# First projections of the two MLPs: feature tiles 8 to 31 by seven products of half-size matrices

## The chip, the cores and the metric

The kernel runs on one core of one Trainium2 chip. The metric is the device time of one execution in microseconds, the median of several executions. A profile is one execution with the hardware profiler on.

## What is computed

The program is a decoder trunk of two residual layers over 512 tokens with 1024 channels. Each layer has a token mixer (gated linear attention and block-sparse attention in the first layer, a short convolution and a pooling mixer in the second) and an MLP with 4096 hidden features. All data is float32. The change touches the MLPs alone:

```python
def rmsnorm(x, g):
    y = x * lax.rsqrt(jnp.mean(x * x, axis=-1, keepdims=True) + EPS)
    return y * g

def mlp(h, w1, w2):                       # w1: (1024, 4096), w2: (4096, 1024)
    a = jax.nn.relu(h @ w1)
    return (a * a) @ w2

for i in range(2):
    x = x + mix_i(rmsnorm(x, norm_mix[i]))
    x = x + mlp(rmsnorm(x, norm_mlp[i]), w1[i], w2[i])
```

## The kernel before

Activations lie transposed: channels on the 128 partitions, the 512 tokens along the free axis, so x is eight tiles of 128x512. The norm's gain is applied before the projection and its scale per token (rs) after it, since the scale is the same for all channels of a token.

**Three matmuls for one product.** Every float32 operand is kept as two float32r parts, hi (a rounded copy) and lo (the rest). `mm3` (L129 to L132) issues three matmuls for one product of tiles: hi times hi (L130), hi times lo (L131), lo times hi (L132). Each has a 128x128 stationary operand (the weights, loaded by a weight load of its own) and 512 moving columns.

**Weight blocks.** The weights come from HBM as blocks of 128x1024 float32 (512 KB) in exactly the order in which PE uses them. `block_parts` (L101) makes one block: SP issues the load into a `raw` buffer (L113), ScalarE casts it to `whi` (L114), VectorE subtracts that from `raw` into `wlo` (L115). There are four buffers each of raw, whi and wlo. `wblock` (L122) gives PE the next block and has two more emitted ahead of it. So ScalarE and VectorE make a block while PE works on earlier ones, and each queue works strictly in its own order.

**The MLP** (`mlp`, from L306). Hidden features are 32 tiles of 128. A unit of the first projection (`t_unit`) makes two feature tiles over eight channel tiles: 2 x 8 x 3 = 48 matmuls of 512 columns from two weight blocks, into one of two PSUM tiles `mm` (two banks each). Its evacuation is four instructions: `r` = max(o, 0) x rs on VectorE (L331), the square on ScalarE (L332), the cast to hi on ScalarE (L334), the subtraction to lo on VectorE (L335). The parts go to slots in A or in E. Four units are a group of eight tiles (`m1(g)`), and a down projection `m2(g)` takes the eight tiles of group g into x: four units of 48 matmuls, each followed by one addition to x (`x_add`, L292). The order is m1(0), m1(1), m2(0), m1(2), m2(1), m1(3), m2(2), m2(3). The last unit of the last MLP is cut into three pieces, the last two of 256 columns, and each piece is added to x (L347) and stored (L348).

**The norm ahead of an MLP.** `Norm.step` splits x times gain into A for each channel tile (hi on ScalarE, lo on VectorE, L259 and L260) and sums squares on POOL (L273). `norm_rs` splits that sum (L278, L279) and has PE add it over the partitions (L280, L281); PE's queue holds these two matmuls behind the MLP's first unit.

Within an MLP POOL has nothing to do before the change.

Of the kernel before, what the change touches and what calls it, by code (L numbers as in the profile page):

```python
# [40 lines left out]
C_N = 128  # L41


@with_exitstack
def kernel(
# [57 lines left out]

    def block_parts(n):
        i = wcount[0]
# [12 lines left out]
    def emit_block():  # L118
        for _ in block_parts(1):
            pass  # L120

    def wblock():  # L122
        while len(ready) < AHEAD + 1 and wcount[0] < w.shape[0]:
            emit_block()
        return ready.pop(0)
# [180 lines left out]
    def mlp(l, nrm, nxt):  # L306
        with ExitStack() as c2:
            mp = c2.enter_context(tc.tile_pool(name=f"mp{l}", bufs=2, reuse_waits="tile"))
            E = mp.tile([P, 16, S], F32R, tag="E", name=f"E{l}", bufs=1)
            st = {}  # L310

            def aslot(f):
                i = f % 8
                if (f // 8) % 2 == 0:
                    return A[:, 16 + i, :], A[:, 24 + i, :]
                return E[:, i, :], E[:, 8 + i, :]

            def apair(f):
                i = f % 8
                if (f // 8) % 2 == 0:  # L320
                    return A[:, 16 + i : 18 + i, :], A[:, 24 + i : 26 + i, :]
                return E[:, i : i + 2, :], E[:, 8 + i : 10 + i, :]

            def m1(g):
                for q in range(4):
                    f = 8 * g + 2 * q
                    o = t_unit(f"m1_{l}_{f}", H)
                    if "rs" not in st:
                        st["rs"] = nrm.rs()
                    r = mp.tile([P, 2, S], F32, tag="r", name=f"r_{l}_{f}")  # L330
                    dve.scalar_tensor_tensor(r, o, 0.0, bc2(st["rs"]), op0=ALU.max, op1=ALU.mult)  # L331
                    act.activation(r, r, AF.Square)  # L332
                    hi, lo = apair(f)
                    act.copy(hi, r)  # L334
                    dve.tensor_sub(lo, r, hi.bitcast(F32))  # L335

            def last_unit(g, n):
                ws = [[t.rearrange("p (k n) -> p k n", k=4) for t in wblock()] for _ in range(2)]
                for j, c0, c1 in ((0, 0, S), (1, 0, S // 2), (1, S // 2, S)):
# [7 lines left out]
                    dve.tensor_add(x[:, row, c0:c1], x[:, row, c0:c1], o[:, c0:c1])  # L347
                    nc.sync.dma_start(out[row * P : (row + 1) * P, c0:c1], x[:, row, c0:c1])  # L348

            def m2(g):  # L350
                for n in range(4):
# [3 lines left out]
                    o = mm_tile(f"m2_{l}_{g}_{n}")  # L355
                    for b in range(2):
# [16 lines left out]

            m1(0)
            m1(1)
            m2(0)
            m1(2)
            m2(1)
            m1(3)
# [724 lines left out]
```

## Time and profile before

| | us |
|---|---|
| median of 3 runs | 1081.18 (1079.22 to 1081.26) |
| profiled execution, its own time | 1080.98 |
| its span, first to last instruction | 1079.2 |
| PE busy in it (matmuls) | 1072.1 |
| PEld busy (weight loads, beside matmuls) | 885.7 |
| DVE busy (VectorE) | 546.0 |
| ACT busy (ScalarE) | 411.7 |
| POOL busy (GpSimd) | 102.4 |

The rows of matmuls are pipelined: one reads 0.39 us long while the next starts 0.23 us after it. What a matmul costs is therefore read from start to start. The same holds in a smaller measure for ScalarE and VectorE, whose rows overlap by about a tenth of a microsecond when they follow each other without a wait. "Landing" of a transfer is the time from the start of its issue to its completion.

### The profile page before, as it was taken

What the parts mean: (1) busy time and instruction counts of PE and PEld (TensorE: products, weight loads), DVE (VectorE), ACT (ScalarE), POOL (GpSimd) and SP (SyncE); (2) the same over time, 40 slices, a digit from 0 to 9 for tenths busy, and PEclk for the clock granted to TensorE, in tenths of its full rate; (3) what the DMA queues carried; (4) which work ended last, traced back from release to release, by engine and by line L of the source; (5) the groups of instructions that cost most, each with busy time, mean ns of one, the idle gap of its engine ahead of it and who ended that gap; (6) DMA issues with size and microseconds to landing.
All of it is one profiled execution on the core that took longest, in us unless ns stands there. A gap on an engine that the chain in (4) does not pass through costs nothing.

```text
span 1079.2 us, 12499 instructions
## 1 busy us (share of the span) xinstructions
PE 1072.1 (99%) x4970; PEld 885.7 (82%) x4970; DVE 546.0 (51%) x767; ACT 411.7 (38%) x597; POOL 102.4 (9%) x113
## 2 busy tenths in 40 slices
PE   9999999999999999999999999999999999999998
PEld 7778888788888888888888888888888888888887
DVE  7788885676444344334334864555443344344331
ACT  6565575755342133124123333334342133133110
POOL 0244432012000000000002100121000000000000
PEclk9999999999999999999999999999999999999999
DMA  8123123123322323333233232332333322322221
GB/s 305 43 78 103 54 90 126 60 78 98 98 98 98 98 98 98 97 98 98 98 98 98 89 97 98 98 98 98 98 98 98 97 98 97 96 96 94 94 72 59
DMA packets 31179, 104.77 MB, mean 97 GB/s; under 512 B 3633, under 2 KB 4498, under 8 KB 31122
## 3 DMA queue, kind: packets, MB, share of 16 engines
q1 hardware_dynamic: 30050, 101.46, 28.8%
q0 software_dynamic: 640, 2.10, 0.6%
q8 instruction: 39, 0.64, 0.3%
q10 hardware_dynamic: 432, 0.42, 0.1%
q14 instruction: 18, 0.15, 0.0%
HBM read 101.87 MB, written 2.10 MB: 96 GB/s over the span
## 4 chain that ended last, share of the span: by engine, by line
PE 95%; DVE 2%; ACT 1%; DMA 0%; issue 0%; DVEq 0%; ACTq 0%
PE m L130 22%; PE m L132 22%; PE m L131 21%; PE wo L130 1%; PE wo L132 1%; PE wo L131 1%; PE av L726 1%; PE ptp L707 1%; PE kb L130 1%; PE kb L132 1%; PE kb L131 1%; PE va L130 1%; PE va L132 1%; PE xc L130 1%; PE va L131 1%; PE xc L132 1%
## 5 line engine op out<-in xcount | busy, mean ns | idle before, releaser
L114 ACT CAST whi<-raw 128x1024 fp32r<-128x1024 f32 (+1 forms) x188 | 194.1, 1034 | 528.0 <-PE m L131 432.0
L115 DVE TENSOR_TENSOR wlo<-raw,whi 128x1024 fp32r<-128x1024 f32 (+1 forms) x188 | 227.2, 1209 | 191.6 <-ACT whi L114 191.5
L132 PE MATMUL m<-A,wlo 128*128 128x512 f32 x768 | 298.8, 389 | 0.0
L131 PE MATMUL m<-A,whi 128*128 128x512 f32 x768 | 298.8, 389 | 0.0
L130 PE MATMUL m<-A,whi 128*128 128x512 f32 x768 | 298.8, 389 | 0.0
L132 PEld LDWEIGHTS m<-A,wlo 128*128 128x128 f32 x768 | 144.2, 188 | 30.1
L130 PEld LDWEIGHTS m<-A,whi 128*128 128x128 f32 x768 | 144.2, 188 | 29.8
L131 PEld LDWEIGHTS m<-A,whi 128*128 128x128 f32 x768 | 144.2, 188 | 29.7
L131 PE MATMUL m<-E,whi 128*128 128x512 f32 (+1 forms) x264 | 101.0, 383 | 0.0
L132 PE MATMUL m<-E,wlo 128*128 128x512 f32 (+1 forms) x264 | 101.0, 383 | 0.0
L130 PE MATMUL m<-E,whi 128*128 128x512 f32 (+1 forms) x264 | 101.0, 383 | 0.0
L292 DVE TENSOR_TENSOR x<-x,m 128x1024 f32<-128x1024 f32 x31 | 37.8, 1221 | 109.1 <-PE m L132 109.1
L331 DVE SCALAR_TENSOR_TENSOR r<-m,rs_n 128x1024 f32<-128x1024 f32 x32 | 39.2, 1224 | 96.8 <-PE m L132 96.8
L273 POOL TENSOR_TENSOR ss_n<-ss_n,sq_n 128x512 f32<-128x512 f32 x21 | 32.8, 1561 | 418.5 <-ACT sq_n L271 417.8
L131 PEld LDWEIGHTS m<-E,whi 128*128 128x128 f32 x264 | 49.6, 188 | 9.8
L132 PEld LDWEIGHTS m<-E,wlo 128*128 128x128 f32 x264 | 49.6, 188 | 9.7
L130 PEld LDWEIGHTS m<-E,whi 128*128 128x128 f32 x264 | 49.6, 188 | 9.5
L332 ACT ACTIVATE r<-r 128x1024 f32<-128x1024 f32 x32 | 34.0, 1062 | 19.9 <-DVE r L331 19.9
L335 DVE TENSOR_TENSOR E<-r,E 128x1024 fp32r<-128x1024 f32 x16 | 19.6, 1226 | 17.2 <-ACT E L334 17.2
L260 DVE SCALAR_TENSOR_TENSOR A<-x,vc,A 128x512 fp32r<-128x512 f32 x24 | 27.3, 1140 | 1.3
L335 DVE TENSOR_TENSOR A<-r,A 128x1024 fp32r<-128x1024 f32 x16 | 19.6, 1225 | 15.1 <-ACT A L334 15.1
L131 PE MATMUL wo<-A,whi 128*128 128x512 f32 x64 | 24.9, 389 | 0.0
(303 smaller groups left out, 1401.7 us busy)
## 6 DMA issues: line engine op xcount, KB each, us to landing
raw<-in_w_dram SPq DMA_DIRECT2D x180, 512.0 KB, 3.3
raw<-in_w_dram SPq DMA_DIRECT2D x8, 256.0 KB, 5.3
x<-in_xT_dram POOLq DMA_DIRECT2D x8, 256.0 KB, 5.8
xin<-in_xT_dram SPq DMA_DIRECT2D x7, 256.0 KB, 5.5
out_dram<-x SPq DMA_DIRECT2D x7, 256.0 KB, 2.1
cd<-in_cond_dram SPq DMA_DIRECT2D x1, 608.0 KB, 6.3
pw<-in_poolw_dram ACTq DMA_DIRECT2D x1, 256.0 KB, 2.5
out_dram<-x SPq DMA_DIRECT2D x2, 128.0 KB, 1.7
```

The source lines that it names most:

```text
L114: act.copy(hi[:, c], raw[:, c])
L115: dve.tensor_sub(lo[:, c], raw[:, c], hi[:, c].bitcast(F32))
L130: pe.matmul(o, w_hi, a_hi, start=start, stop=False)
L131: pe.matmul(o, w_hi, a_lo, start=False, stop=False)
L132: pe.matmul(o, w_lo, a_hi, start=False, stop=stop)
L260: dve.scalar_tensor_tensor(A[:, 8 + k, c], src[:, k, c], col(gcol + k), A[:, k, c].bitcast(F32), op0=ALU.mult, op1=ALU.subtract)
L273: (pool if buf is None else dve).tensor_add(ss, ss, sq)
L292: dve.tensor_add(x[:, 2 * n : 2 * n + 2, :], x[:, 2 * n : 2 * n + 2, :], o)
L331: dve.scalar_tensor_tensor(r, o, 0.0, bc2(st["rs"]), op0=ALU.max, op1=ALU.mult)
L332: act.activation(r, r, AF.Square)
L335: dve.tensor_sub(lo, r, hi.bitcast(F32))
L707: pe.transpose(tp[:, c : c + P], hs[h, i][:, j * P : (j + 1) * P], ident)
```

## The change

Feature tiles 0 to 7 are projected as before, in four units. The other 24 tiles are made in six groups of four tiles (`m1_sevenths`). In a group the weights are seen as a 2 x 2 matrix of blocks (two halves of the channels, even and odd channel tiles; two halves of the features), the activations likewise (the two halves of the channels; the first and the last 256 tokens), and the product of the two is formed from seven products of halves where four outputs with two products each would need eight (the form with sums that are used again). One product is 2 x 4 x 3 = 24 matmuls of 256 moving columns from one weight block, so a group has seven weight blocks and 168 matmuls, where four tiles had four weight blocks and 96 matmuls of 512 columns.

The operands of the products are sums:

- Sums of activations: `act_sums` makes four sums per pair of channel tiles, once for each MLP, beside the plain units: two activations and one cast on ScalarE, four additions of 128x256 and one subtraction of 128x1024 on VectorE, four times. They are kept as hi and lo in the new tile Z (zh, zl).
- Sums of weights: of the seven blocks of a group two are plain and the others are sums of up to four blocks, formed by transfers that add to their destination (`accum_op=ALU.add`). POOL issues these, four for each group of 512 KB each; SP issues four plain loads for each group (a, b, y, z). The buffer b goes through three additions: it is split into hi and lo, added to, split again. The buffer y (one buffer, `bufs=1`) goes through one.

The outputs are put together on VectorE and ScalarE: two copies out of PSUM on ScalarE (L434, L436), seven additions and subtractions of 128x512 on VectorE (L440 to L451), and for each half of the group (`finish`) max with 0 and square on ScalarE (L417, L418), cast to hi (L420) and lo on VectorE (L421). rs is no longer applied there: relu(rs z) squared is rs squared times relu(z) squared, so a down projection of groups 1 to 3 multiplies its PSUM result by rs squared (`down`, L459) ahead of the addition to x (L461), one instruction more on VectorE. Numbers L113 and up in this part are lines of the changed file.

The order of an MLP becomes: plain tiles 0 to 7; group 2 (tiles 8 to 11), m2(0); groups 3 and 4, m2(1); groups 5 and 6, m2(2); group 7, m2(3). So of six groups four stand in two pairs, back to back.

```diff
+    def split_w(raw, i):
+        ...
+        act.copy(hi, raw)
+        dve.tensor_sub(lo, raw, hi.bitcast(F32))
+    def sum_block(n):
+        i = wcount[0]
+        if n == 0:
+            first = raw_block(i, 3, "a")
+            sums["b"] = raw_block(i, 3, "b")
+            nc.gpsimd.dma_start(sums["b"], w[i + 2], accum_op=ALU.add)
+            split_w(first, f"{i}_0")
+        elif n == 1:
+            sums["y"] = sums["pool"].tile([P, 1024], F32, tag="sumy", name=f"sumy{i}", bufs=1)
+            nc.sync.dma_start(sums["y"], w[i])
+            split_w(sums["y"], f"{i}_1")
+            nc.gpsimd.dma_start(sums["y"], w[i + 2], accum_op=ALU.add)
+        elif n == 2 or n == 4:
+            split_w(sums["b"], f"{i}_{n}")
+            nc.gpsimd.dma_start(sums["b"], w[i + (n == 4)], accum_op=ALU.add)
+        elif n == 3:
+            split_w(sums["y"], f"{i}_3")
+        elif n == 5:
+            split_w(raw_block(i, 1, "z"), f"{i}_5")
+        else:
+            split_w(sums["b"], f"{i}_6")
+            wcount[0] += 4
...
-            mp = c2.enter_context(tc.tile_pool(name=f"mp{l}", bufs=2, reuse_waits="tile"))
-            E = mp.tile([P, 16, S], F32R, tag="E", name=f"E{l}", bufs=1)
+            mp = c2.enter_context(tc.tile_pool(name=f"mp{l}", bufs=4, reuse_waits="tile"))
+            E = mp.tile([P, 8, S], F32R, tag="E", name=f"E{l}", bufs=1)
+            Z = mp.tile([P, 16 * S + 64], F32R, tag="Z", name=f"Z{l}", bufs=1)
...
+            def act_sums(n):
+                y, s = two(f"y{n}"), two(f"s{n}")
+                for j in range(2):
+                    act.activation(y[:, j, :], x[:, 2 * n + j, :], AF.Copy, scale=col(nrm.gcol + 2 * n + j))
+                ...
+                dve.tensor_sub(s3, h7, h1)
+                dve.tensor_sub(s2, h6, h7)
+                dve.tensor_sub(s4, s3, h6)
+                dve.tensor_add(s5, s4, h0)
+                act.copy(zh[:, n, :], s)
+                dve.tensor_sub(zl[:, n, :], s, zh[:, n, :].bitcast(F32))
...
+            def m1_sevenths(f0):
+                dc = mm_tile(f"dc_{nm}")
+                m4, m7 = dc[:, 0, :], dc[:, 1, :]
+                m1, m5 = (m_tile(f"{i}_{nm}", "s") for i in ("m1", "m5"))
+                ...
+                def finish(j):
+                    act.activation(rr[j], rr[j], AF.Relu)
+                    act.activation(rr[j], rr[j], AF.Square)
+                    hi, lo = (v[:, j::2, :] for v in agroup(f0))
+                    act.copy(hi, rr[j])
+                    dve.tensor_sub(lo, rr[j], hi.bitcast(F32))
+                def product(o, slot):
+                    hi, lo = wblock()
+                    for u in range(2):
+                        for k in range(4):
+                            c = slice((4 * u + k) * P, (4 * u + k + 1) * P)
+                            ah, al = operand(slot, k)
+                            mm3(o[:, u * HALF : (u + 1) * HALF], hi[:, c], lo[:, c], ah, al, k == 0, k == 3)
+                ...
+                product(m4, 5)
+                product(m1, 6)
+                act.copy(c11, wide(m1))
+                product(m5, 2)
+                act.copy(es, wide(m5))
+                product(m7, 3)
+                m6 = m_tile(f"m6_{nm}", "s")
+                product(m6, 4)
+                dve.tensor_add(c21, wide(m6), c11)
+                dve.tensor_sub(c22, wide(m7), c21)
+                dve.tensor_add(c12, c21, es)
+                dve.tensor_add(c21, wide(m4), c22)
+                dve.tensor_sub(c22, c22, es)
+                finish(1)
+                m2_ = m_tile(f"m2_{nm}", "tp")
+                product(m2_, 0)
+                dve.tensor_add(c11, wide(m2_), c11)
+                m3 = m_tile(f"m3_{nm}", "av")
+                product(m3, 1)
+                dve.tensor_add(c12, wide(m3), c12)
+                finish(0)
+            def down(n, g, o, c=slice(0, S), j=slice(0, 2)):
+                xs = x[:, 2 * n : 2 * n + 2, c][:, j]
+                if g > 0:
+                    ...
+                    dve.tensor_mul(t, o, st["rs"][:, None, c].to_broadcast([P, m, c.stop - c.start]))
+                    o = t
+                dve.tensor_add(xs, xs, o)
...
-            m1(0)
-            m1(1)
-            m2(0)
-            m1(2)
-            m2(1)
-            m1(3)
-            m2(2)
-            m2(3)
+            for f in range(0, 8, 2):
+                m1_plain(f)
+            for g, qs in enumerate(((2,), (3, 4), (5, 6), (7,))):
+                for q in qs:
+                    m1_sevenths(4 * q)
+                    if q == 2:
+                        dve.tensor_mul(st["rs"], st["rs"], st["rs"])
+                m2(g)
```

In m2(3) the first halves of units 0 and 1 also come ahead of their second halves, and the list of weight blocks (`_layout`) is rearranged to match.

What the queues hold is shown at two places. In names such as `whi56_4` the first number is the block's place in the list of weights (52 and 56 are the pair of groups 3 and 4 in the first MLP) and the second is the product, 0 to 6; `r12_0` and `r12_1` are the two halves of the outputs of the group that starts at tile 12.

ScalarE's queue before, around the evacuation of tiles 12 to 15:

```order
L332 ACTIVATE r_0_12_3013<-r_0_12_3013 128x1024
L334 CAST E0_2540<-r_0_12_3013 128x1024
L114 CAST whi50_3086<-raw50_3085 128x1024
L114 CAST whi51_3116<-raw51_3115 128x1024
L332 ACTIVATE r_0_14_3079<-r_0_14_3079 128x1024
L334 CAST E0_2540<-r_0_14_3079 128x1024
L114 CAST whi52_3148<-raw52_3147 128x1024
L114 CAST whi53_3178<-raw53_3177 128x1024
```

ScalarE's queue now, from the end of the first group of the pair into the second:

```order
L417 ACTIVATE r12_1_0_3352<-r12_1_0_3352 128x1024
L418 ACTIVATE r12_1_0_3352<-r12_1_0_3352 128x1024
L417 ACTIVATE r12_0_0_3351<-r12_0_0_3351 128x1024
L420 CAST A_82<-r12_1_0_3352 128x2x512
L418 ACTIVATE r12_0_0_3351<-r12_0_0_3351 128x1024
L113 CAST whi56_3_3617<-sumy56_3546 128x1024
L420 CAST A_82<-r12_0_0_3351 128x2x512
L434 COPY r16_0_0_3585<-m1_0_16_3583 128x2x256
L113 CAST whi56_4_3646<-raw56_b_3513 128x1024
L113 CAST whi56_5_3678<-raw56_z_3676 128x1024
L436 COPY es_0_16_3587<-m5_0_16_3584 128x512
L113 CAST whi56_6_3707<-raw56_b_3513 128x1024
```

Two casts of weights stood between the evacuations of two units; now the six instructions that finish a group, one cast and one copy stand ahead of the fifth cast of the next group.

POOL's queue before, where the norm ahead of the first MLP ends and the one behind it begins:

```order
L273 TENSOR_TENSOR ss_n1_84<-ss_n1_84,sq_n15_2487 128x512
L273 TENSOR_TENSOR ss_n1_84<-ss_n1_84,sq_n16_2524 128x512
L273 TENSOR_TENSOR ss_n1_84<-ss_n1_84,sq_n17_2529 128x512
L273 TENSOR_TENSOR ss_n2_2536<-ss_n2_2536,sq_n21_4423 128x512
L273 TENSOR_TENSOR ss_n2_2536<-ss_n2_2536,sq_n22_4490 128x512
```

POOL's queue now, in the pair of groups 52 and 56 of the first MLP (x2 is two in a row):

```order
L126 DMA raw52_b_3285<-in_w_dram 128x1024
L126 DMA raw56_b_3513<-in_w_dram 128x1024
L132 DMA sumy52_3316<-in_w_dram 128x1024
L135 DMA raw52_b_3285<-in_w_dram 128x1024 x2
L132 DMA sumy56_3546<-in_w_dram 128x1024
L135 DMA raw56_b_3513<-in_w_dram 128x1024 x2
```

Where POOL went from one norm to the next, it now issues eight adding transfers for a pair, 24 for each MLP, each behind the split that reads its buffer.

## Rows read from the trace of the kernel before

**Rows 1.** The page: busy time of each engine over the span with its share and count; TensorE's granted clock in 40 slices (9 is nine tenths or more); the share of each engine in the chain that ended last.

```profile
PE 1072.1 (99%) x4970; PEld 885.7 (82%) x4970; DVE 546.0 (51%) x767; ACT 411.7 (38%) x597; POOL 102.4 (9%) x113
...
PEclk9999999999999999999999999999999999999999
...
PE 95%; DVE 2%; ACT 1%; DMA 0%; issue 0%; DVEq 0%; ACTq 0%
```

**Rows 2.** The waits of PE over the span, the three longest of six (the other three sum to 0.8): its line, who it waited for, microseconds in total, times, the longest.

```profile
PE warmup L394 <- DVE warm L78: 1.2, 1, 1.2
PE tp_k L487 <- DVE kl L497: 1.0, 1, 1.0
PE kb L130 <- ACT A L259: 0.6, 1, 0.6
...
```

**Rows 3.** PE in order of time (start us, duration us, engine, line, operation, shape) in a down projection, 512 moving columns. Between the first row and the last lie 35 MATMUL rows.

```profile
1054.95 0.39 PE L130 MATMUL m<-E,whi 128*128 128x512 f32 x1
...
1063.11 0.39 PE L130 MATMUL m<-E,whi 128*128 128x512 f32 x1
```

**Rows 4.** The same view in the last down projection, whose last two pieces have 256 moving columns: the first and the last of 48 MATMUL rows of that width, two weight loads (PEld) between them, and the VectorE addition behind the last.

```profile
1069.91 0.28 PE L130 MATMUL m<-E,whi 128*128 128x256 f32 x1
...
1071.23 0.19 PEld L130 LDWEIGHTS m<-E,whi 128*128 128x128 f32 x1
1071.35 0.19 PEld L131 LDWEIGHTS m<-E,whi 128*128 128x128 f32 x1
...
1075.54 0.28 PE L132 MATMUL m<-E,wlo 128*128 128x256 f32 x1
1075.86 0.42 DVE L347 TENSOR_TENSOR x<-x,m 128x256 f32<-128x256 f32 x1 [2.46 <-PE m L132]
```

**Rows 5.** Groups of instructions by line and form on ScalarE: count, then busy us and mean ns of one, then idle time before them and what ended it.

```profile
L114 ACT CAST whi<-raw 128x1024 fp32r<-128x1024 f32 x180 | 189.3, 1053 | 526.6 <-PE m L131 432.0 <-PE wo L131 23.6 <-PE xc L131 13.3
L332 ACT ACTIVATE r<-r 128x1024 f32<-128x1024 f32 x32 | 34.0, 1062 | 19.9 <-DVE r L331 19.9
L455 ACT COPY kr<-kb 128x512 f32<-128x512 f32 x2 | 1.2, 586 | 2.4 <-PE kb L132 2.4
```

**Rows 6.** The same view of VectorE.

```profile
L115 DVE TENSOR_TENSOR wlo<-raw,whi 128x1024 fp32r<-128x1024 f32 x180 | 221.7, 1232 | 191.4 <-ACT whi L114 191.3
L335 DVE TENSOR_TENSOR E<-r,E 128x1024 fp32r<-128x1024 f32 x16 | 19.6, 1226 | 17.2 <-ACT E L334 17.2
L252 DVE SCALAR_TENSOR_TENSOR t_n<-nps_n,t_n 128x512 f32<-128x512 f32 x4 | 2.8, 690 | 0.1
L347 DVE TENSOR_TENSOR x<-x,m 128x256 f32<-128x256 f32 x2 | 0.8, 421 | 4.6 <-PE m L132 4.6
```

**Rows 7.** Instructions in order of time where the engine has work queued: two in a row on ScalarE, then two in a row on VectorE.

```profile
204.41 1.05 ACT L114 CAST whi<-raw 128x1024 fp32r<-128x1024 f32 x1
205.37 0.69 ACT L850 ACTIVATE ob<-ob,osm 128x128 f32<-128x128 f32 x2
...
230.83 1.22 DVE L292 TENSOR_TENSOR x<-x,woa 128x1024 f32<-128x1024 f32 x1 [5.80 <-PE woa L132]
231.97 1.22 DVE L115 TENSOR_TENSOR wlo<-raw,whi 128x1024 fp32r<-128x1024 f32 x1
```

**Rows 8.** Line 113 on SP's queue (the weight blocks, 512 KB each but for eight of 256 KB): duration of one issue in ns, count, first and last start, and the time from issue to landing.

```profile
L113 SPq DMA_DIRECT2D raw<-in_w_dram x188: 327/328/473, 0.7 to 1034.4; - x188
...
DMA to landing us min/median/max: 3.1/3.4/8.1
```

**Rows 9.** The same view of line 777, eight transfers of 256 KB that POOL issues one behind the other; the last row is the landing of the first of them alone.

```profile
L777 POOL DMA_DIRECT2D x<-in_xT_dram x8: 536/537/748, 159.0 to 162.9; - x8
...
DMA to landing us min/median/max: 3.9/5.8/6.4
...
DMA to landing us min/median/max: 3.9/3.9/3.9
```

**Rows 10.** DMA queues in three windows of half a microsecond, 160.0 to 160.5, 160.5 to 161 and 161.5 to 162 us (q0 is POOL's queue, q1 SP's): packets, MB, share of 16 engines. The first of POOL's transfers moves its bytes here.

```profile
q1 hardware_dynamic: 45, 0.18, 94.9%
...
q0 software_dynamic: 16, 0.07, 49.4%
q1 hardware_dynamic: 39, 0.10, 49.4%
...
q0 software_dynamic: 37, 0.13, 96.3%
```

**Rows 11.** Three stretches of 1 us around the transfer of one weight block: busy time of each engine with its count, granted clock, DMA share and GB/s.

```profile
302.00:303.00 1.00, 1.00 (x6) 0.81 (x5) 0.28 (x1) 0.69 (x1) 0.00 (x0) 1.00 0.36 70
303.00:304.00 1.00, 1.00 (x6) 0.84 (x5) 0.94 (x1) 0.00 (x0) 0.00 (x0) 1.00 0.96 344
304.00:305.00 1.00, 1.00 (x7) 0.81 (x6) 0.00 (x0) 0.50 (x1) 0.00 (x0) 1.00 0.28 111
```

**Rows 12.** Start of the first MLP in order of time: its first MATMUL, VectorE's low half of the sum of squares (L279), and the second MATMUL of the norm (L281), which reads that half.

```profile
244.23 0.39 PE L130 MATMUL m<-A,whi 128*128 128x512 f32 x1
...
252.04 0.69 DVE L279 TENSOR_TENSOR ss_n<-ss_n,ss_n 128x512 fp32r<-128x512 f32 x1 [1.83 <-ACT ss_n L278]
...
255.34 0.39 PE L281 MATMUL nps_n<-ss_n,ones_r 128*128 128x512 f32 x1
```

More of the change, by code (lines that the diff above doesn't have):

```diff
@@ L41 @@
 C_N = 128
+LEAN = 48
 @with_exitstack
@@ L118, in emit_block @@
     def emit_block():
-        for _ in block_parts(1):
-            pass
+        if todo[0] is None:
+            for _ in block_parts(1):
+                pass
+        else:
+            sum_block(todo.pop(0))
     def wblock():
-        while len(ready) < AHEAD + 1 and wcount[0] < w.shape[0]:
+        while len(ready) < AHEAD + 1 and todo:
             emit_block()
@@ L324, in m1 @@
[L324 to L335, printed above, removed]
+                return [t[:, f % 4, :] for t in agroup(f)]
@@ new lines, in operand, with m1_plain @@
+            def operand(slot, k):
+                if 2 <= slot <= 5:
+                    c = slice((slot - 2) * HALF, (slot - 1) * HALF)
+                    return zh[:, k, c], zl[:, k, c]
+                r = 2 * k + (slot < 2)
+                c = slice(HALF, S) if slot == 1 else slice(0, HALF)
+                return A[:, r, c], A[:, 8 + r, c]
+            def m1_plain(f):
+                o = t_unit(f"m1_{l}_{f}", H)
+                if f == 0:
+                    act_sums(0)
+                    st["rs"] = nrm.rs()
+                r = two(f"r{f}")
+                dve.scalar_tensor_tensor(r, o, 0.0, bc2(st["rs"]), op0=ALU.max, op1=ALU.mult)
+                act.activation(r, r, AF.Square)
+                hi, lo = (t[:, f % 4 : f % 4 + 2, :] for t in agroup(f))
+                act.copy(hi, r)
+                dve.tensor_sub(lo, r, hi.bitcast(F32))
+                for n in {2: (1, 2), 4: (3,)}.get(f, ()):
+                    act_sums(n)
@@ L980, with _order, _group @@
     mlp(1, n3, None)
+def _order():
+    m1, m2 = tuple(range(7)), 8 * (None,)
+    mlp = 8 * (None,) + m1 + m2 + 2 * m1 + m2 + 2 * m1 + m2 + m1 + m2
+    return 32 * (None,) + mlp + 24 * (None,) + mlp
+def _group(np, blocks, w, f0):
+    v = w.reshape(4, 2, P, w.shape[1])
+    for j in range(2):
+        for h in range(2):
+            c = [v[:, h, :, (f0 + 2 * u + j) * P : (f0 + 2 * u + j + 1) * P] for u in range(2)]
+            blocks.append(np.stack(c).transpose(2, 0, 1, 3).reshape(P, 1024))
 def _t_block(np, w, k0, n0, width):
```

86 lines of the change are left out of this document (57 added, 29 removed).

## The prediction

> **What bounds the kernel now.** I read the page first: PE is busy 99% of the span, the granted clock stands at nine tenths or more in all 40 slices, and PE has 95% of the chain that ended last [rows 1]. The list of PE's waits next: the longest is 1.2 us and all six together 3.6 us [rows 2]. So the kernel runs at the speed of its matmuls at full clock (2.4 GHz); no wait is left to win. Then the matmuls in order of time, for the price of one at either width: 36 intervals of 512 columns take 8.16 us, 0.2267 us each [rows 3]; 47 intervals of 256 columns take 5.63 us, 0.120 us each [rows 4]. Last, what the other engines pay for a block of weights: 1.05 us of ScalarE and 1.23 us of VectorE [rows 5, 6], where PE uses it for 24 x 0.2267 = 5.44 us. They are about half idle, and each transfer fills the DMA engines for a short part of that time only [rows 11].
>
> **The change, part by part.**
>
> *Matmuls.* A group of four tiles took 96 x 0.2267 = 21.76 us and takes 168 x 0.120 = 20.16 us, 1.60 us less. One eighth fewer columns would give 2.72; 168 starts at a little more than half price give back the rest. Twelve groups: -19.2 us. A product now lasts 24 x 0.120 = 2.88 us, so a new pair of hi and lo is due every 2.88 us instead of every 5.44.
>
> *ScalarE and VectorE by their sums.* Where work is queued, a 128x1024 instruction follows the last after 0.96 us on ScalarE and 1.14 us on VectorE [rows 7], about 0.09 less than it reads [rows 5, 6]. In a group ScalarE has seven casts, two copies of 128x512 (0.586 less 0.09, 0.5 each) and six instructions in `finish`: 7 x 0.96 + 2 x 0.5 + 6 x 0.97 = 13.5 us. VectorE has seven subtractions for weights, seven of 128x512 (0.690 less 0.09, 0.60 each) and two in `finish`: 7 x 1.14 + 7 x 0.60 + 2 x 1.14 = 14.5 us. Both lie under 20.16, so no engine becomes the bound by its sum; what counts is order, below.
>
> *Sums of activations.* Four times four additions of 128x256 (0.421 less 0.09, about 0.34) and one subtraction of 1.14 are 10 us of VectorE in each MLP, beside four plain units of 10.88 us. Only `act_sums(0)`, emitted ahead of `nrm.rs()`, can be late: about 2.5 us now stand before the low half of the squares, which ended at 252.04 + 0.69 = 252.73 while its matmul came at 255.34 [rows 12]. That leaves 2.6 us; I take 0, with 2.5 us as the other bound.
>
> *Down projections.* One multiplication of 1.14 us on VectorE more in each unit of groups 1 to 3: hidden behind units of 10.88 us, with two PSUM buffers. In the very last piece nothing hides it: one more instruction of 0.42 [rows 4], +0.45 with its start. The squaring of rs comes once for each MLP and is hidden. PE's blocks in m2(3) come in another order and cost nothing.
>
> *Plain loads.* A group has four on SP and lands them in 3.1 to 3.4 us as a rule [rows 8]; two others are queued ahead, so nothing waits for them.
>
> *Adding transfers.* No row of before shows one. Four come with each group, issued by POOL, whose queue is in order. The nearest rows are POOL's plain transfers of 256 KB: the first, alone, is issued at 159.0 and lands after 3.9 us [rows 9]. Its bytes appear between 160 and 160.5 at the earliest and run at 0.13 MB in half a microsecond, 262 GB/s [rows 10]: 1.5 us ahead of the bytes, 1.0 for 256 KB, so about 1.4 behind them, of which I count 1.1, since the first bytes come a little before the window shows them. For 512 KB the lower bound is then 1.5 + 2.0 + 1.1 = 4.6 us, if an add moves what a copy moves. If the destination has to be read as well, twice the bytes pass, 4.0 us, and it lands after 6.6. Beside a plain load, which takes the DMA engines for 0.36 + 0.96 + 0.28 = 1.6 us [rows 11], that is 8.2. The bounds are 4.6 and 8.2; I take 6.4, the middle, which is also the worst landing of POOL's eight in a row [rows 9].
>
> The Trainium skill ("Collectives: The Full Stack", section "The bandwidth ceiling: the fold count and why AG ≠ RS ≠ AR") says that an addition in the DMA datapath needs two source reads and that such a step ran at about half the rate of a copy. No transfer of before adds, so no row bears on it; by that page's ratio the estimate would be the 6.6 just worked out, and the sum about 3 us worse than mine (four second groups at some 3.0 instead of 2.2 us each).
>
> *Where an add is waited for.* Buffer b goes through split, add, split, add, split: a split is a cast and a subtraction, about 2.3 us from landing to the end of the low half. Products come in the order 0 to 6, and product n is due n x 2.88 us after the group starts; product 6 at 17.28. Let F be the start of the first group of a pair and L the landing time, 6.4. In the first group the second add is issued at F-2.9 and lands at F+3.5; the split ends at F+5.8 (product 4, due F+11.5); the third add lands at about F+12.3, its split ends at F+14.6. Due F+17.28: 2.7 us to spare. In the second group of the pair (start G = F+20.16) the same chain meets the end of the first. The order shown for ScalarE has all six instructions of `finish` and a cast of weights ahead of the copy of m1 and `whi56_4`: seven of 0.97 and one of 0.5 from G+0.8 end at G+8.2. VectorE, ahead of `wlo56_2`, has two subtractions of weights and six of 0.60, 5.9 us, which end at G+0.7; `wlo56_2` at G+1.9, so the second add can land at G+8.3. `whi56_4` follows at once, the split ends at G+10.65, the third add lands at G+17.1, and its split ends at G+19.4. Due at G+17.28: PE waits about 2.2 us. There are four second groups in the program: +8.8 us. The first and single groups follow a down projection with its long units, and have no such queue.
>
> The same walk at other landings gives for each second group: 5.5 or less, 0; 6.0, 0.8; 7.0, 4.6 (two landings stand in the chain, so it grows by about two for one, less what ScalarE's queue hides); 7.5, 6.6; 8.0, about 8, and first groups begin to wait as well.
>
> *Sum.* Profiled execution 1080.98, 0.2 below the median of the runs shown; -19.2 (matmuls), +8.8 (adds in second groups), +0.45 (tail), 0 (the rest): **1071.0 us**.
>
> **Rivals.**
>
> *B: the adds land late.* At 7.5 us (destination read too, and half of the adds share with a plain load) second groups wait 6.6 us each, 26.4 together, and the last block of the single group ahead of m2(3) some 1.4 us in each MLP: 1080.98 - 19.2 + 26.4 + 2.8 + 0.45 = 1091; with the sharing less often, 1088. It decides from a landing of about 7.0 us, where 4 x 4.6 = 18.4 eats the gain. For it: the bound of 8.2 and a median landing of 5.8 for only 256 KB when transfers queue [rows 9]. Against it: the DMA engines move 70 and 111 GB/s around a block's transfer [rows 11] and are mostly free.
>
> *C: adds as quick as copies.* At a landing of 5.5 or less nothing waits: 1080.98 - 19.2 + 0.45 = 1062.2. For it: the lower bound of 4.6. It is on the side of my forecast.
>
> *D: a weight load bounds a narrow matmul.* PEld rows read 0.19 us long; if 256 columns could not hide that, a group would take 168 x 0.188 = 31.6 us and the program 12 x 9.8 = 118 us more, 1199. Against it stand the rows themselves: two weight loads start 0.12 us apart, and 48 narrow matmuls went at 0.120 each [rows 4]. That was in a run of only 48; I leave it little.
>
> *E: another queue than the adds'.* ScalarE's or VectorE's order, or the first MLP's norm, costs several microseconds that I put at nothing. Of this kind the 2.5 us at the norm is the one I can price; a product waiting 1 us in each of twelve groups would be 12, and give 1083.
>
> **How the numbers follow.** My forecast with landings from 5.5 to 6.8, 1062 to 1077: 0.42. C, 1061 to 1064: 0.20. Landings from 6.8 to 7.2, or E in part, give 1078 to 1084: 0.12. B, 1085 to 1092: 0.18. Beyond 1092, later landings still or D: 0.08. The range is 1061 to 1092. About 0.2%, 2.2 us, is what a measurement of this kernel can tell from no change. Faster by more (below 1079.0): the first two and a little of the third, 0.64. Within 0.2% (1079.0 to 1083.3): 0.10. Slower: 0.26.
>
> **What would show it.** Matmuls `dc` and `m` of 256 columns: 0.12 us apart inside a product, and a group without waits 20.2 us from first to last. The landings of POOL's issues in `sum_block`: 6.4 by my forecast, 7.5 by B, 5.5 or less by C. PE's waits: by my forecast about 2 us each, four times, on the hi and lo of product 6 of the second group of each pair and nowhere else in the MLPs; none by C; 5 us and more there, and some in single groups, by B. A wait of the norm's second matmul near the start of an MLP would be the 2.5 us that I left out. At the end two VectorE instructions of 0.42 behind the last matmul. The granted clock stays at nine tenths or more if waits are short; should it fall behind one, the matmuls after it will cost more than counted here. The forecast is wrong if adds land outside 5.5 to 6.8, or if PE waits in groups where no queue of `finish` stands ahead of a split.

## The result and the profile after

The changed kernel takes 1068.43 us, the median of four executions (1063.26 to 1069.19), where the kernel before took 1080.21 beside it: a ratio of 0.9881, 95% interval 0.9847 to 0.9914. Forecast were 1071.0 us, in a range of 1061 to 1092. The profiled execution is the fastest of the four, 1063.26 us with a span of 1061.5; the other three have spans of 1066.6 to 1067.4 and a mean granted clock of 0.996 to 0.998 where the profiled one has 1.0. So two things are to be explained: the 17.7 us between the two profiled executions, and the 5 us that the other three add.

The page of the profile after: engines with busy us, share and count, granted clock in 40 slices, DMA queues (packets, MB, share of 16 engines; q0 is POOL's), and POOL's transfers with their median us from issue to landing.

```profile
PE 1046.9 (99%) x5834; PEld 903.4 (85%) x5834; DVE 661.7 (62%) x931; ACT 492.2 (46%) x705; POOL 142.3 (13%) x161
...
PEclk9999999999999999999999999999999999999999
...
q1 hardware_dynamic: 30050, 101.46, 29.3%
q0 software_dynamic: 7552, 27.27, 15.0%
...
raw_b<-in_w_dram POOLq DMA_DIRECT2D x36, 512.0 KB, 5.5
...
sumy<-in_w_dram POOLq DMA_DIRECT2D x12, 512.0 KB, 5.7
```

PE is busy 1046.9 us instead of 1072.1 [rows 1], 25 less, where the prediction counted 19 less. The matmuls say why. PE in order of time: the first and the last of 24 on Z (`dc`), the first and the last of 24 on A (`m`), both in the first group of a pair, then the first matmul of the second group, and the first and the last of a later product on Z in it.

```profile
350.89 0.28 PE L174 MATMUL dc<-Z,whi 128*128 128x256 f32 x1
...
353.60 0.28 PE L176 MATMUL dc<-Z,wlo 128*128 128x256 f32 x1
353.72 0.28 PE L174 MATMUL m<-A,whi 128*128 128x256 f32 x1
...
356.47 0.28 PE L176 MATMUL m<-A,wlo 128*128 128x256 f32 x1
...
370.51 0.29 PE L174 MATMUL dc<-Z,whi 128*128 128x256 f32 x1
...
378.85 0.28 PE L174 MATMUL dc<-Z,whi 128*128 128x256 f32 x1
...
381.46 0.28 PE L176 MATMUL dc<-Z,wlo 128*128 128x256 f32 x1
```

On A they start 2.75 / 23 = 0.120 us apart, as in [rows 4]. On Z it is 2.71 / 23 = 0.118 in the first product of a group that follows long matmuls and about 2.61 / 23 = 0.1135 in the others. Four of the seven products read Z, and a group without a wait lasts 370.51 - 350.89 = 19.62 us, not 20.16.

The waits of PE, after, the four longest:

```profile
PE m L174 <- ACT whi L113: 3.1, 3, 1.6
PE m L176 <- DVE wlo L114: 3.0, 4, 0.8
PE m L175 <- DVE A L304: 1.3, 1, 1.3
PE warmup L526 <- DVE warm L79: 1.2, 1, 1.2
```

The first two are new and stand on product 6 of the four second groups alone, 2.37, 1.92, 0.75 and 1.05 us. The third is the first unit of the first MLP. The first of the four places: PE in order of time (the bracket is the idle time and who ended it), then ScalarE, POOL and SP around it (SP's row holds three issues, of which the first starts at 381.34), and the time from issue to landing of POOL's last transfer.

```profile
387.03 0.28 PE L176 MATMUL m<-A,wlo 128*128 128x256 f32 x1
388.93 0.39 PE L174 MATMUL m<-A,whi 128*128 128x256 f32 x1 [1.62 <-ACT whi L113]
389.15 0.28 PE L175 MATMUL m<-A,whi 128*128 128x256 f32 x1
390.19 0.38 PE L176 MATMUL m<-A,wlo 128*128 128x256 f32 x1 [0.75 <-DVE wlo L114]
```

```profile
376.45 1.04 ACT L420 CAST A<-r 128x1024 fp32r<-128x1024 f32 x1
377.39 0.57 ACT L434 COPY r<-m 128x512 f32<-128x512 f32 x1
377.87 1.05 ACT L113 CAST whi<-raw_b 128x1024 fp32r<-128x1024 f32 x1
...
387.83 1.04 ACT L113 CAST whi<-raw_b 128x1024 fp32r<-128x1024 f32 x1 [7.49 <-DMA raw_b<-in_w_dram]
```

```profile
372.00 0.87 POOL L135 DMA_DIRECT2D raw_b<-in_w_dram  x1 [2.06 <-DVE wlo L114]
380.47 0.88 POOL L135 DMA_DIRECT2D raw_b<-in_w_dram  x1 [7.60 <-DVE wlo L114]
```

```profile
381.34 10.89 SPq L154 DMA_DIRECT2D raw<-in_w_dram  x3
```

```profile
DMA to landing us min/median/max: 7.3/7.3/7.3
```

The second group starts at 370.51. The second add is issued at 372.00 and lands after 5.5 us, at 377.5; the cast of block 4 starts at 377.87. The third is issued at 380.47, a plain load follows 0.87 us later on SP's queue, and this add lands after 7.3 us (last line). ScalarE stands idle until then, and PE behind it. In the other three second groups the plain load follows at the same distance, and the third add lands after 5.96, 6.00 and 5.96 us.

At the end two VectorE instructions of 0.42 us follow the last matmul (1057.69 and 1058.15), where one stood [rows 4].

The sum of the 17.7 us, from first to last matmul of each MLP: 348.39 us before and 342.37 after in the first, 348.80 and 338.74 in the second, so 16.1 less; the end takes 0.5 more. Another 2.1 less lies ahead of the first MLP, in code that didn't change: in the profiled execution of before, the first projection's matmuls started 0.43 us apart until 9.5 us and 0.23 from there, while after they reached 0.23 at 6.3. Executions of the kernel before lie at 1079.2 or near 1081, and the profiled one was of the longer kind.

### The profile page after: what moved, and what is told of

It is laid out like the page before. It is cut to its first block, busy times and chain, and to the rows that moved or that the text cites. A ratio compares the mean times of both kernels' runs of the same rounds, so it can differ in the third digit from the quotient of the medians.

```text
span 1061.5 us, 14621 instructions
## 1 busy us (share of the span) xinstructions
PE 1046.9 (99%) x5834; PEld 903.4 (85%) x5834; DVE 661.7 (62%) x931; ACT 492.2 (46%) x705; POOL 142.3 (13%) x161
## 3 DMA queue, kind: packets, MB, share of 16 engines
q0 software_dynamic: 7552, 27.27, 15.0%
## 5 line engine op out<-in xcount | busy, mean ns | idle before, releaser
L174 PE MATMUL m<-A,whi 128*128 128x512 f32 (+1 forms) x808 | 282.4, 350 | 3.1 <-ACT whi L113 3.1
L176 PE MATMUL m<-A,wlo 128*128 128x512 f32 (+1 forms) x808 | 282.4, 349 | 3.0 <-DVE wlo L114 3.0
L175 PE MATMUL m<-A,whi 128*128 128x512 f32 (+1 forms) x808 | 282.0, 349 | 1.3 <-DVE A L304 1.3
L155 ACT CAST whi<-raw 128x1024 fp32r<-128x1024 f32 (+1 forms) x140 | 142.3, 1024 | 200.1 <-PE m L175 106.0
L156 DVE TENSOR_TENSOR wlo<-raw,whi 128x1024 fp32r<-128x1024 f32 (+1 forms) x140 | 171.0, 1224 | 58.2 <-ACT whi L155 57.7
L113 ACT CAST whi<-raw_b 128x1024 fp32r<-128x1024 f32 x36 | 37.8, 1051 | 99.3 <-DMA raw_b<-in_w_dram 56.7
L459 DVE TENSOR_TENSOR t<-m,rs_n 128x1024 f32<-128x1024 f32 (+2 forms) x26 | 29.7, 1141 | 65.8 <-PE m L176 65.8
L113 ACT CAST whi<-sumy 128x1024 fp32r<-128x1024 f32 x24 | 25.2, 1049 | 62.8 <-PE m L175 62.8
L174 PE MATMUL dc<-Z,whi 128*128 128x256 f32 x192 | 53.4, 278 | 0.0
L175 PE MATMUL dc<-Z,whi 128*128 128x256 f32 x192 | 53.3, 278 | 0.0
L176 PE MATMUL dc<-Z,wlo 128*128 128x256 f32 x192 | 53.3, 278 | 0.0
L174 PE MATMUL m<-Z,whi 128*128 128x256 f32 x192 | 53.1, 277 | 0.0
L175 PE MATMUL m<-Z,whi 128*128 128x256 f32 x192 | 53.1, 276 | 0.0
L176 PE MATMUL m<-Z,wlo 128*128 128x256 f32 x192 | 53.0, 276 | 0.0
L174 PE MATMUL m<-E,whi 128*128 128x512 f32 x128 | 49.8, 389 | 0.0
L175 PE MATMUL m<-E,whi 128*128 128x512 f32 x128 | 49.8, 389 | 0.0
L176 PE MATMUL m<-E,wlo 128*128 128x512 f32 x128 | 49.8, 389 | 0.0
```

The costliest lines, as they stand in the source:

```text
L113: act.copy(hi, raw)
L155: act.copy(hi[:, c], raw[:, c])
L156: dve.tensor_sub(lo[:, c], raw[:, c], hi[:, c].bitcast(F32))
L174: pe.matmul(o, w_hi, a_hi, start=start, stop=False)
L175: pe.matmul(o, w_hi, a_lo, start=False, stop=False)
L176: pe.matmul(o, w_lo, a_hi, start=False, stop=stop)
```

## The experiments

**The same kernel again.**

> The changed kernel once more, unchanged. The profile of the changed kernel reads 1063.26 us at a granted clock of 1.0; three executions without one read 1068.4 to 1069.2 with a mean granted clock of 0.996 to 0.998. Theory: a wait of PE of about 2 us (in the profile two second groups wait 2.4 and 2.0) is now and then long enough for the clock to fall, and that is the other 5 us; then a profile that reads about 1068 shows the granted clock below 1.0 right behind a wait on the low or high half of product 6 of a second group. Rival: the clock falls at a place that has nothing to do with the change (the start, the mixers).

Measured: 1064.48 us (1063.44 to 1067.5). The profiled execution is the one of 1067.5, at a mean clock of 0.998; the others lie at 1063.4 to 1064.8 with 1.0. Its clock fell at one place ahead of the program's end. Windows there: busy time of PE, PEld, DVE, ACT, POOL with counts, granted clock, DMA share, GB/s.

```profile
473.00:476.40 3.40, 0.50 (x5) 0.30 (x3) 0.00 (x0) 1.01 (x2) 0.00 (x0) 1.00 0.13 48
476.40:478.00 1.60, 0.76 (x4) 0.56 (x5) 1.54 (x2) 1.60 (x3) 0.00 (x0) 0.98 0.00 0
478.00:481.30 3.30, 3.30 (x17) 3.30 (x17) 3.30 (x6) 1.27 (x2) 0.00 (x0) 0.50 0.65 181
481.30:483.00 1.70, 1.70 (x12) 1.53 (x12) 1.70 (x3) 0.94 (x1) 0.00 (x0) 0.99 0.76 265
```

```profile
476.48 0.38 PE L174 MATMUL m<-A,whi 128*128 128x256 f32 x1 [2.98 <-ACT whi L113]
```

PE waited 2.98 and 0.76 us for product 6 of a second group (its third add landed after 8.2 us), and from 478.0 the clock stood at 0.50, 1.2 GHz, to 481.3; matmuls there start 0.213 us apart. 3.3 us at half speed cost 1.7 us. This pair lasts 44.89 us, where the same pair lasted 41.56 in the profile without the fall. In this one profile the theory holds.

**Where Z starts.** `LEAN` moves the start of the sums in Z, which together with A, E and the weights would otherwise lie 192 bytes past a multiple of 512:

```diff
-LEAN = 48
+LEAN = 0        # 16 and 32 in two further runs
```

> LEAN is 0 instead of 48, so the sums of activations in Z start 192 bytes past a multiple of 512 as A, E and the weights do, and not at 384. In the profile of the changed kernel matmuls of 256 columns that read Z start 0.1135 us apart and those that read A 0.120. Theory: the address does that; all four products on Z then cost 24 x 0.120, a group 20.16 instead of 19.61, twelve groups 6.6 us more, of which the waits in second groups give back up to 2 (their blocks are due later): 1064 to 1070 in a profile without a fall of the clock. Rival: what is read (Z's layout or its users) makes the difference, and the time stays.

> LEAN is 16: Z's sums start at 256 past a multiple of 512, which is a multiple of 128 and 64 bytes away from where the weights start. If a multiple of 128 is what counts, products on Z cost 0.1135 apart as with 48; if the distance to the weights' own start counts, anything between 0.1135 and 0.120.

> LEAN is 32: Z's sums start at 320 past a multiple of 512, no multiple of 128, 128 bytes away from where the weights start. If a multiple of 128 counts, products on Z cost 0.120 as those on A; if any distance from the weights' start will do, 0.1135.

Measured: 1068.12 us (1066.83 to 1069.17) with 0, one execution each at 1064.92 with 16 and 1064.62 with 32. With 0 the first and last matmul of a product on Z:

```profile
380.30 0.28 PE L174 MATMUL dc<-Z,whi 128*128 128x256 f32 x1
...
383.06 0.28 PE L176 MATMUL dc<-Z,wlo 128*128 128x256 f32 x1
```

2.76 / 23 = 0.120: the address makes the difference. A group without a wait lasts 20.15 us, the 20.16 of the prediction. With `LEAN` at 16 the matmuls on Z start 0.1178 apart, at 32 they start 0.1187 apart in steady stretches. A start at a multiple of 128 bytes is not what counts: 16 and 48 both give one (256 and 384 past a multiple of 512), and they read 0.1178 and 0.1135.

**A and E, or the weights, moved as Z was.**

```diff
-    A = cp.tile([P, 32, S], F32R, name="A")
+    A_ = cp.tile([P, 32 * S + 128], F32R, name="A")
+    A = A_[:, LEAN : LEAN + 32 * S].rearrange("p (k n) -> p k n", k=32)     # leanA; E likewise
```

```diff
     A = cp.tile([P, 32, S], F32R, name="A")
+    cp.tile([P, 48], F32, name="gap")                                       # wshift: what follows moves
```

> A and E start 192 bytes later (at 384 past a multiple of 512, as Z's sums do), with the weights where they were. Both theories give the same here: 2,856 matmuls of 512 columns on A and E at about 0.220 instead of 0.2267 (-19 us), 911 of 256 columns on A at 0.1135 instead of 0.120 (-5.6 us). Blocks fall due earlier by 0.4 us in a group, so waits in second groups may grow by 2 us in all: about 1040, well under both kernels. If the gain of Z is something of its own, nothing changes: 1062 to 1068.

> The buffers of weights (raw, whi, wlo) start 192 bytes later: at 384 past a multiple of 512, with A left at 192; E is then at 384 and Z's sums at 64. Starts of 256-column matmuls so far: 0.120 with Z at 0 bytes from the weights' start, 0.1178 at 64, 0.1187 at 128, 0.1135 at 192, each past a multiple of 512. Theory (a): the distance from the weights counts. Matmuls that read A are then 192 away and faster: 0.1135 at 256 columns, about 0.220 instead of 0.2267 at 512; those that read E (now at the weights' own distance) stay at 0.2267; Z as fast as before. 2,600 rows of 512 columns by 0.0067 and 900 of 256 by 0.006 are about 22 us less: near 1042. Theory (b): the moving operand's own start counts. Then A stays at 0.120 and 0.2267, E (384) falls to 0.220, Z (64) rises towards 0.119: near 1064.

Measured: leanA 1081.51 us (1077.75 to 1086.88), ratio to the kernel before 1.0017 (1.0001 to 1.0033); wshift 1072.41 (1070.96 to 1073.76). Both expectations of a gain failed, and for one reason. In leanA 256 columns on A do fall to 0.1135 us. But here are two matmuls of a down projection with 35 between them:

```profile
319.65 0.39 PE L176 MATMUL m<-A,whi 128*128 128x512 f32 x1
...
328.05 0.39 PE L176 MATMUL m<-A,whi 128*128 128x512 f32 x1
```

8.40 / 36 = 0.2333 us instead of 0.2267 [rows 3]: what helps the short matmuls harms the long ones, and 2,856 long ones by 0.0067 are 19 us. In wshift the long ones on A, whose own start hadn't moved, take 0.2301 us on the mean in the first MLP and 0.2290 in the second, against 0.2269 and 0.2268 in the changed kernel, so (b) falls. Those on E, which had moved with the weights, settle at 0.2267 but take 0.2287 on the mean, with slower ones behind each change from A to E. (a) has the direction wrong for the long ones on A, and products on Z stood mostly at 0.1177, where it wanted 0.1135.

**More starts.** A 64 bytes from the weights' place, E 128 (first MLP) and 256 (second), Z 256 and 32, one execution.

> Starts of tiles only, the same work: A 64 bytes, E 128 (first MLP) and 256 (second), Z's sums 256 (first MLP) and 32 (second) past the weights' own place in 512 bytes. So far at 0, 64, 128 and 192: 0.120, 0.1178, 0.1187 and 0.1135 us with 256 columns; at 0 and 192: 0.2267 and 0.233 with 512. If 512 columns follow what 256 do with the sign turned, A and E read 0.229 to 0.232 here; if 192 bytes alone are slow, 0.227 or less. Nothing of the prediction hangs on it: it says whether any place is better for the long matmuls than the one they have.

Measured: 1072.38 us. Long matmuls, on the mean of each MLP: 0.229 us on A, 0.2323 on E at 128, 0.2286 on E at 256 (where they settle at 0.2267). Short ones on Z: 0.120 at 256, 0.117 at 32. No place tried was better for the long ones than the one they have. Short ones on A, at one and the same start, read 0.118 in the first MLP and 0.1135 in the second, so the start alone is not the rule either.

**The adds as copies.**

```diff
-            nc.gpsimd.dma_start(sums["b"], w[i + 2], accum_op=ALU.add)
+            nc.gpsimd.dma_start(sums["b"], w[i + 2])          # and so the other two lines
```

> POOL's 48 transfers don't add, they overwrite; so the sums of weights are left out and the outputs of the MLPs are not the reference's. All instructions and waits are the same. The adds landed after 5.2 to 7.3 us (median 5.5). Theory: the landing of the adds is what the second groups wait for; a copy of 512 KB lands after about 4.6 us by the bound of the prediction, two landings stand in the chain, so 1.8 us of each wait go: second groups wait 0 to 0.6 and the profile reads about 1057 to 1058, with no fall of the clock. Rival: an add costs what a copy costs (landing still 5.5), and the waits stay; then 1061 to 1067.

Measured: 1055.54 us (1055.46 to 1055.74), ratio 0.9778 (0.9765 to 0.979). POOL's queue in its page:

```profile
q0 software_dynamic: 7552, 27.27, 8.3%
...
raw_b<-in_w_dram POOLq DMA_DIRECT2D x36, 512.0 KB, 3.8
```

A copy is issued in 0.53 us and lands after 3.8; an add takes 0.87 and 5.5. No wait of PE is left in any group: pairs last 39.14 to 39.29 us, about twice a group (of the MLPs' waits only the 1.3 us of the first unit stays). So the second groups wait for nothing but what the slower landings of the adds cause. The second copy and the cast of block 4, in the second group that starts at 370.83:

```profile
371.67 0.53 POOL L135 DMA_DIRECT2D raw_b<-in_w_dram  x1 [2.41 <-DVE wlo L114]
```

```profile
377.53 1.06 ACT L113 CAST whi<-raw_b 128x1024 fp32r<-128x1024 f32 x1
```

The copy lands at 371.67 + 3.8 = 375.5, and the cast comes 2 us later, 6.70 us after the group: this is what ScalarE's queue alone allows. With adds the second landing comes 6.96 us after the group, a little later than that.

**The first finish of a pair later.**

```diff
+                for j in late:          # behind product(m5, 2) of the second group:
+                    j()                 # finish(1), finish(0) of the first
```

> In each pair the first group's finish (six instructions on ScalarE, two on VectorE) comes behind the second group's third product. The prediction named this queue as the reason that the cast of block 4 (whi56_4) comes late. In the profile of the changed kernel that cast started 7.36 us after the group, and the add that it needs had landed at about 7.0. If ScalarE's queue were the cause, the waits of 2.4, 2.0, 0.8 and 1.1 us would go and the profile read about 1056. Rival: the landings and VectorE's queue ahead of the second split set the pace, and the cast gains no more than 0.4 us: waits fall by 0.4 each, 1060 to 1062 (or 1065 to 1068 where the clock falls).

Measured: 1059.6 us (1059.38 to 1059.86), ratio 0.9815 (0.9802 to 0.9828), no clock below 0.999. The waits of second groups fall from 6.1 to 3.3 us, more than the rival and less than the theory allowed, and not for the reason that either gave. ScalarE again, then SP:

```profile
377.83 1.03 ACT L113 CAST whi<-raw_b 128x1024 fp32r<-128x1024 f32 x1
...
381.14 1.05 ACT L113 CAST whi<-raw_z 128x1024 fp32r<-128x1024 f32 x1
...
385.91 1.05 ACT L113 CAST whi<-raw_b 128x1024 fp32r<-128x1024 f32 x1 [3.24 <-DMA raw_b<-in_w_dram]
```

```profile
383.66 6.05 SPq L154 DMA_DIRECT2D raw<-in_w_dram  x3
```

The cast of block 4 starts as late as before (377.83, 377.87), 0.1 us behind the landing of its add: ScalarE's queue was not what held it. But a step of the finish now stands ahead of the cast of `raw_z`, so that buffer comes free 2.3 us later, and the plain load that takes it starts 3.2 us behind the third add and not 0.87. That add lands after 5.5 us instead of 7.3; in the other three second groups the third adds land after 5.97, 5.34 and 5.31 instead of 5.96, 6.00 and 5.96.

**Low halves last.**

```diff
-                            mm3(o[:, u * HALF : (u + 1) * HALF], hi[:, c], lo[:, c], ah, al, k == 0, k == 3)
+                            pe.matmul(half, hi[:, cs[k]], ah, start=k == 0, stop=False)
+                            pe.matmul(half, hi[:, cs[k]], al, start=False, stop=False)
+                        for k in range(4):
+                            ah, al = operand(slot, k)
+                            pe.matmul(half, lo[:, cs[k]], ah, start=False, stop=k == 3)
```

> In each half of a product the eight matmuls with the high half of the weights come first and the four with the low half last (same 24 matmuls). The low half of product 6 is so wanted 0.96 us after the product starts and not 0.24. Theory: in each second group the last 0.8 us of PE's wait is for that low half (0.8, 0.8, 0.8, 0.8 in the profile of the changed kernel); these 3 us go, the waits for the high half (1.6, 1.2 and 0.3) stay, and where a wait was long enough for the clock to fall it may still fall: about 1060 in a profile without a fall, against 1063.3. Rival: the order of hi and lo reads costs as much in the matmuls as it saves.

Measured: 1080.46 us (1077.05 to 1082.59), ratio 0.9999 (0.9989 to 1.0009). The whole gain is gone, and the matmuls are not the cause: a group without a wait still lasts 19.62 us. ScalarE in the same second group, which starts at 371.07:

```profile
375.63 1.05 ACT L113 CAST whi<-sumy 128x1024 fp32r<-128x1024 f32 x1 [6.67 <-DMA sumy<-in_w_dram]
376.58 2.00 ACT L417 ACTIVATE r<-r 128x1024 f32<-128x1024 f32 x2
378.49 1.99 ACT L418 ACTIVATE r<-r 128x1024 f32<-128x1024 f32 x2
380.39 1.98 ACT L420 CAST A<-r 128x1024 fp32r<-128x1024 f32 x2
382.27 0.57 ACT L439 COPY r<-m 128x512 f32<-128x512 f32 x1
382.75 1.04 ACT L113 CAST whi<-raw_b 128x1024 fp32r<-128x1024 f32 x1
```

The order of ScalarE's queue came out otherwise: the cast that waits for an add into `sumy` now stands ahead of all six instructions of the finish, and they stand ahead of the cast of block 4, which starts 11.7 us after the group and not 7.4. PE waits for a high half twice in each second group, 14.7 us in all, the clock falls once in each pair, and pairs last 44.9 to 45.7 us. Here the queue that the prediction had named does decide, because the finish itself stands behind a landing.

**Three edits together, and two.** The first sums of activations move behind the norm's steps:

```diff
                 if f == 0:
-                    act_sums(0)
                     st["rs"] = nrm.rs()
-                for n in {2: (1, 2), 4: (3,)}.get(f, ()):
+                for n in {0: (0,), 2: (1, 2), 4: (3,)}.get(f, ()):
```

> Three edits together: the finish of a pair's first group behind the second group's third product (which measured 1059.6), the low halves last in each half product, and the first sums of activations behind the norm's own steps. By the parts: 1059.6 less 2.4 (waits for low halves) less 1.3 (the wait for A's last low half at the first MLP's start): about 1056, with no fall of the clock. If the third add then decides through its landing alone, 0.9 of that stays in the one wait for a high half. If sums of activations are late where they now stand, PE waits for Z at the first group of seven products.

> Two edits: a pair's first finish behind the second group's third product (alone 1059.6), and the first sums of activations behind the norm's own steps. Theory: the sums between the splits of A on VectorE are what delays A's last low half by 1.3 us at the first MLP's start; that wait goes, the rest stays: about 1058.3, with no fall of the clock. Rival: the wait at the start was there for the order of the norm's steps themselves, and nothing changes (1059.6); or the sums now stand ahead of the first evacuation and PE waits for its PSUM tile instead.

Measured: 1060.74 us (1058.93 to 1060.99), ratio 0.9821 (0.9808 to 0.9835), with all three; 1058.04 (1057.08 to 1058.2), ratio 0.9794 (0.978 to 0.9808), with the two. The wait of 1.3 us at the first MLP's start is gone in both, so the sums on VectorE were its cause. Low halves last bring nothing beside the later finish: waits of 1.5 us in all for a copy out of PSUM on ScalarE take the place of those for low halves. The version with two edits beats both kernels.

## Why the prediction came out as it did

- **What bounds the kernel:** right. PE is busy 99% before and after, and of the other engines only what delays a block of weights shows.
- **Matmuls, -19.2 us:** right in kind, too small. A group lasts 19.62 us without a wait, 2.14 less than 21.76: -25.7 for twelve. The step that failed took 0.120 from the one place where short matmuls stood [rows 4] for all of them. The changed kernel has 64 spare columns in Z and starts its sums 48 columns in; I gave that no price. Without the offset, lean0 has the group that I had counted (20.15 us, 20.16 counted).
- **Adds in second groups, +8.8 us:** right in place, and nearly in size, the size partly by luck. The four pairs last 42.03, 41.56, 40.44 and 40.71 us, 7.8 more than eight groups of 19.62; single groups wait for nothing. The landing is 5.5 us at the median and not 6.4. For 5.5 my list of other landings gave no wait, but that was an error in its working: the walk itself, redone at 5.5, has the cast of block 4 at G+8.2, its split done at 10.55, the third landing at 16.05 and its split done at 18.35, 1.1 us past the 17.28 at which I had product 6 due. (At 7.5 it gives 4.3 us, where the list has 6.6.) Product 6 is also due earlier, 16.64 us after its group as plain shows, and so the walk comes to 1.7 us each, 6.8 together. And the third add lands after 6.0 us in three of the four places and after 7.3 in the other, up to 8.2 in again: the upper bound of the prediction, which I had left to rival B.
- **The cause of that wait:** partly wrong. I let ScalarE's finish hold the cast of block 4 to 8.2 us after the group. In the first of the four places it started at 7.36, and at most 0.4 of that was the queue (0.4 to 0.7 in the others); the landing of the second add set it, and VectorE's queue ahead of the split of block 2, behind which that add is issued. plain shows that the queue alone would have let it go at 6.70. defer shows that a lighter queue doesn't bring it forward, and lolast shows what the queue costs where it does decide.
- **Sums of activations, 0 with a bound of 2.5:** 1.3 us, and at A's last low half in the first unit instead of the norm's second matmul. all and defer_sums remove it.
- **The tail, +0.45:** right (0.46 between the two instructions' starts).
- **The clock:** named as a thing that could go wrong, not priced. A fall costs 1.7 us, and where the changed kernel's clock fell in a profile (again) it fell behind the longest wait. That execution is 4.2 us longer than the profiled one of the result: 1.7 for the fall and 2.3 for longer waits in second groups. That the other executions with a mean clock below 1.0 are longer for the same reason is likely and not shown, since what they waited for is not recorded.
- **Rivals:** C fell, since PE waits at landings of 5.3 to 5.5 (defer); its condition came from the error in that list, and the profiled execution's 1063.26 us stand near its 1062.2 by another sum. B fell by its landing: the median is 5.5 us, and only two of the eight third adds in second groups reached its 7.5 in the two profiles of the changed kernel. These eight, each with a plain load 0.87 us behind it, landed after 5.8 to 8.2 us, the four of defer, with the load 3.2 us behind, after 5.3 to 6.0; why the same distance gives 6 once and 8 another time stays open. D fell: 19.62 us a group. Rival E came true in one place, the 1.3 us of the sums of activations.
- **The number:** 1071.0 us against a median of 1068.43 is closer than the parts are. For the profiled execution 6.5 too little was taken off for matmuls, 1.0 too much was added for second groups, 1.3 was left out at the first MLP's start, and 2.1 lie in the unchanged start: 1071.0 - 6.5 - 1.0 + 1.3 - 2.1 = 1062.7, against 1063.26. The other three executions, some 5 us longer, bring the median back towards the forecast, and the prediction had no term for that: luck.

An add holds the DMA engines for nearly twice the time of a copy: POOL's queue takes the 16 engines for 15.0% of 1061.5 us with adds and for 8.3% of 1053.8 with copies, and its 27.27 MB read the same in both pages. That is (159 - 87) / 48 = 1.5 us more for each add, on 1.7 for a copy (87 us for 27.27 MB, 52 times 512 KB). The Trainium skill ("Collectives: The Full Stack", section "The bandwidth ceiling: the fold count and why AG ≠ RS ≠ AR") puts an addition, in a step of a collective, at two source reads and about half the rate of a copy; these shares agree with the rate (3.2 us against 1.7), and no row here shows the second read. The landing of 6.6 us that I worked out from it was 1.1 too long, 0.8 of it because my bound for a copy was 4.6 and a copy lands after 3.8.

## What to carry to other kernels

Where a transfer adds to a buffer that is split, added to and split again, the chain of landings is the thing to lay against the consumer's pace: a chain with slack behind long units has none between two groups back to back. Look at what a late step frees, too: a buffer that comes free earlier starts a load that can run beside the one you wait for. And an edit that changes only the order on one engine may reorder another's queue: read the queues again before you price it.

## What the runs showed of the hardware

The same matmul costs more or less with the place at which its operands start. With 256 moving columns of float32r it was 0.1135 to 0.120 us, with 512 columns 0.2267 to 0.2333, and the start that was best for the one was worst for the other (lean0, leanA, the profile after). The distance between the starts of the moving operand and of the weights is part of it, since matmuls on A changed their price when the weights moved and A did not (wshift). But neither it nor the moving operand's own start orders all cases (wshift, map), and at one start Z read 0.118 in the first product behind long matmuls and 0.1135 elsewhere. The rule stays open.

The clock fell behind a wait of 2.98 and 0.76 us on one product (again), of 1.52 and 0.76 (lean0), and of 2.26 to 2.51 at one stretch (four times in lolast). It did not fall behind 1.62 and 0.75 (the profile after) nor behind 1.78 and 0.76 (an earlier pair in again). So two waits of 2.3 to 2.5 us in all went either way.
